# A four-branch encoder trunk in split float32: merged products reordered, down projections accumulated onto 2h in PSUM, a later first quad, and other PSUM banks

## The chip, the cores and the metric

The kernel runs on one core of a Trainium2 chip. The metric is the device time of one execution in microseconds, the median of several. A profile of one execution goes with it: for every instruction of the five engines (PE, the matrix engine, with its weight loads PEld; DVE, the vector engine; ACT, the scalar engine; POOL; SP) its start, its duration and what it waited for.

## The reference

```python
D_MODEL, SEQ, DEPTH, D_FF, CONV_DIM, N_HEADS = 1024, 512, 2, 2816, 512, 8
for i in range(DEPTH):
    h = h + 0.5 * swiglu(rmsnorm(h, ffn1_norm[i]), ffn1_w_gu[i], ffn1_w_down[i])
    u = rmsnorm(h, mix_norm[i])
    b_g, c_g, v_c, q_c, kv_c, k_r, g_conv, g_mla = split(u @ w_in[i])
    y_conv = (b_g * causal_conv3(c_g * v_c)) @ w_conv_out[i]
    y_mla = mla_branch(q_c, kv_c, k_r, ...)         # 8 heads, rotary keys, chunk mask
    h = h + (sigmoid(g_conv) * y_conv + sigmoid(g_mla) * y_mla) @ w_o[i]
    h = h + 0.5 * swiglu(rmsnorm(h, ffn2_norm[i]), ffn2_w_gu[i], ffn2_w_down[i])
    h = h + sigmoid(rmsnorm(h, ple_norm[i]) @ w_ple_gate[i]) * (p[i] @ w_ple_proj[i])
return rmsnorm(h, final_norm)
# swiglu(x): g, u = split(x @ w_gu); (silu(g) * u) @ w_down
```

All of it is float32, for 512 frames of 1024 channels.

## The kernel before

**Numbers and tiles.** `h` stands in SBUF as eight tiles of 128 channels by 512 frames. Every product is done in split precision: a value is the sum of a high and a low part (`wh`, `wl` for weights; `...h`, `...l` for activations), and `mm3` adds three matmuls, high by high (line 279), high by low (280), low by high (281), into one PSUM bank of 512 float32 columns. Weights come in blocks of 128 by 1024 (eight 128x128 tiles), by a DMA on SP's queue into one of ten buffers `st`. ACT makes the high part of a block (line 71) and DVE the low part (line 72). There are four buffers for each of the two, so a block is split at most four blocks ahead of the PE.

**Quads.** Most columns of the FFN's gate and up weights, and the mixer's gates, go through a seven-product scheme for 2x2 blocks (`Sevens`). A quad `n` makes four 128-column groups. Its seven products are named 1 to 7 and are run by `step(n, j)`. DVE forms sums of weight quarters (lines 150 to 168, tiles `st` and `s`) and of activations (`Halved.row`: for each of four `j` the sums `t` and `u` and their splits). Products 1, 2, 4, 6, and also 3 where the quad isn't "early", are merged ones, done by `joint`: for each of eight pairs of k and w, a 512-column matmul of the high weights with both parts of the activation (line 530) and then a 256-column matmul of the low weights (line 532). Products 5 and 7 (and an early 3) are done by `product` with 24 matmuls of 256 columns (line 542). ACT copies a chain's partial sum from one PSUM tile to another so that two results go on from it: `seed`, line 548. `out` and `finish` turn a result into activations.

**FFN.** `ffn(l, nm, name, first, beside, early)` is called as a0 and a1 (first FFN of layers 0 and 1) and b0, b1 (second). There are 22 column groups: in a0 four of them are done as whole products (`n_whole = 4`) and nine quads follow; in a1 it is two and ten quads; in b0 and b1 all eleven are quads, and the first two are early. `next_quad(n)` runs the rest of quad `n` among the first products of quad `n + 1`. At the places marked `None`, `fill()` puts in one down projection `down(m, f0, f0 + 4)`: twelve matmuls of 512 columns into a bank, which DVE then adds at half weight to `h[m]` (line 665). The last downs close the FFN. In a0, `beside` is `rotary`, which makes the cosine and sine tables: two DMAs on ACT's queue, 27 DVE instructions (lines 417 to 437) and two on ACT. It is called once, between the last downs.

**Mixer, per-layer embedding.** `mixer(l)` (tiles m0, m1) does the key/value and query latents (`kvp`, `qp`), the conv branch (`Cp`, `Vp`, `Bp` for k = 0 to 3), four quads of gates, then attention (`Pair`: `q_rope`, `keys_queries`, `values`; `scores`; `turn`; `mix_v`). `ple(l)` (tiles e0) does gate and projection for eight m, each pair into two banks.

**PSUM.** There are eight banks. `banks.paired()` makes three pools: `chain` (`PB`: two tiles of two banks), `seeded` (`PA`: one tile of two banks) and `single` (`PS`: two banks). `banks.eight()` makes eight single banks, for attention. A tile of a new pool waits until the old tile on its bank has been read.

**Order.** The program is traced in the order of the Python code. A planner then orders each engine's instructions at compile time, by that order as priority and by its own estimates of when data and buffers are there. On the chip each engine runs its list in order.

Of the kernel before, what the change touches and what calls it, by code (L numbers as in the profile page):

```python
# [16 lines left out]
P = 128  # L17
# [176 lines left out]
def trunk_kernel(ctx, tc, dims, x, p, positions, gains, rope_c, final_row, weights, out):  # L194
# [79 lines left out]
            nc.scalar.activation(hi, src, AF.Copy, scale=scale)  # L274
            return nc.vector.scalar_tensor_tensor(lo, src, scale, hi.bitcast(F32), ALU.mult, ALU.subtract)

    def mm3(ps, w, v, first, last):
        (wh, wl), (vh, vl) = w, v
        nc.tensor.matmul(ps, wh, vh, start=first, stop=False)  # L279
        nc.tensor.matmul(ps, wh, vl, start=False, stop=False)  # L280
        nc.tensor.matmul(ps, wl, vh, start=False, stop=last)  # L281

    def proj(tiles, vs, name, ps=None):
        ps = PS(name) if ps is None else ps
# [126 lines left out]
    def rotary():  # L411
        rc = cp.tile([P, 2], F32, tag="rc", name="rc")
        nc.scalar.dma_start(out=rc, in_=rope_c)
        pos_i = gp.tile([P, S], I32, tag="g", name="pos_i")
        nc.scalar.dma_start(out=pos_i, in_=positions.to_broadcast([P, S]))
# [5 lines left out]
        nc.vector.tensor_scalar(turns, ang, 1.0 / (2 * math.pi), None, ALU.mult)  # L421
        nc.vector.tensor_scalar(big, turns, 2.0 ** -15, magic, ALU.mult, ALU.add)
        nc.vector.tensor_scalar(big, big, magic, None, ALU.subtract)
        nc.vector.scalar_tensor_tensor(turns, big, -(2.0 ** 15), turns, ALU.mult, ALU.add)
        nc.vector.tensor_scalar(sml, turns, magic, None, ALU.add)
        nc.vector.tensor_scalar(sml, sml, magic, None, ALU.subtract)
        c2 = TWO_PI_PARTS
        for n_, c_ in ((big, c2[0] * 2 ** 15), (big, c2[1] * 2 ** 15), (sml, c2[0]), (big, c2[2] * 2 ** 15), (sml, c2[1]),
                       (big, c2[3] * 2 ** 15), (sml, c2[2]), (big, c2[4] * 2 ** 15), (sml, c2[3])):
            nc.vector.scalar_tensor_tensor(ang, n_, -c_, ang, ALU.mult, ALU.add)  # L430
        nc.vector.tensor_scalar(big, ang, 1.0 / (2 * math.pi), magic, ALU.mult, ALU.add)
        nc.vector.tensor_scalar(big, big, magic, None, ALU.subtract)
        for c_ in c2[:3]:
            nc.vector.scalar_tensor_tensor(ang, big, -c_, ang, ALU.mult, ALU.add)
        lim = 3.1415925
        nc.vector.tensor_scalar(ang, ang, lim, -lim, ALU.min, ALU.max)
        nc.vector.scalar_tensor_tensor(big, ang, -1.0, ang, ALU.mult, ALU.min)
        nc.scalar.activation(cosT, big, AF.Sin, bias=hpi)
        nc.scalar.activation(sinT, ang, AF.Sin, scale=rc[:, 1:2])

# [55 lines left out]
    class Sevens:  # L496
# [27 lines left out]
        def joint(self, ps, d, j):  # L524

            hi, lo = d.pop(("part", j), None) or d["w"].part(j)
            for k, (vh, pair) in enumerate(self.ys[j]):
                for w in range(2):
                    at = slice((2 * k + w) * P, (2 * k + w + 1) * P)
                    nc.tensor.matmul(ps[:, w, :].rearrange("p (a t) -> p a t", t=self.H), hi[:, at], pair, start=j == 1 and k == 0,  # L530
                                     stop=False, skip_group_check=True)
                    nc.tensor.matmul(ps[:, w, :self.H], lo[:, at], vh, start=False, stop=k == 3, skip_group_check=True)

        def product(self, ps, d, j, start=False):

# [68 lines left out]

    def ffn(l, nm, name, first=False, beside=None, early=2):

        H = S // 2
        nf = DFF // P
# [50 lines left out]

        def down(m, f0, f1, ps=None, last=True, first_=True):  # L660
            ps = PS(f"{name}pd{f0}_{m}") if ps is None else ps
            for f in range(f0, f1):
                mm3(ps, W.get((nm + "_w_down", l, f * P, m * P)), acts[f], first_ and f == f0, last and f == f1 - 1)
            if last:
                nc.vector.scalar_tensor_tensor(h[m], ps, 0.5, h[m], ALU.mult, ALU.add)  # L665
            return ps

        np_ = nf // 2
# [19 lines left out]
        if n_whole == 0:  # L688
            x_ins, sums = ys.other(KD // 2 - 1, xs)

            with tc.issue_after(x_ins):
                step(0, 1)
                step(0, 5)
            r = rms(acc, D, name)
            with tc.issue_after(x_ins):
                step(1, 1)
                step(1, 5)
            behind = sums
            for n, j in ((0, 2), (0, 6), (0, 3), (0, 7), (1, 2), (0, 4), (1, 6), (1, 3), (1, 7)):
                with tc.issue_after(behind):  # L700
# [3 lines left out]
        else:  # L704
# [19 lines left out]
                ys.row(j, xs)  # L724
            activate(n_whole - 2)
            f = n_whole - 1
            step(n0, 1)
            pss[f] = [proj(cs[f][0], xs, f"{name}pg{f}")]
            step(n0, 2)
            step(n0, 6)  # L730
            pss[f].append(proj(cs[f][1], xs, f"{name}pu{f}"))
            step(n0, 5)
            activate(f)
            step(n0, 7)
            step(n0, 3)
            if first:
                downs.extend((m, 0) for m in range(KD))
        for n in range(n0, np_ - 1):
            next_quad(n)

# [28 lines left out]
    def mixer(l):  # L769
# [296 lines left out]
    def ple(l):  # L1066
# [11 lines left out]
            nc.vector.tensor_tensor(h[m], h[m], g, ALU.add)  # L1078

        for m in range(KD):  # L1080
            pg, pp = halves((PA if m % 3 == 2 else PB)(f"{name}gp{m}"))
            proj(W.col("w_ple_gate", l, m * P, D), xs, None, pg)
            proj(W.col("w_ple_proj", l, m * P, PD), pt, None, pp)
            pss.append((pg, pp))
# [165 lines left out]
                store(1, 0, hg[1], nc.sync)  # L1250

    for l in range(DEPTH):
        ffn(l, "ffn1", f"a{l}", l == 0, rotary if l == 0 else None, 2 if l else 0)
        mixer(l)
        ffn(l, "ffn2", f"b{l}", early=3)
        (ple_last if l == DEPTH - 1 else ple)(l)
# [48 lines left out]
```

## Time and profile before

| | |
|---|---|
| median of 3 runs | 2321.09 us (2320.75 to 2321.31) |
| the profiled execution | 2320.87 us, of which the span from first to last instruction is 2318.8 us |
| PE busy | 2273.8 us, 98% (12272 matmuls) |
| PE weight loads | 1960.4 us, 85% |
| DVE busy | 1853.1 us, 80% |
| ACT busy | 1270.3 us, 55% |
| DMA | 223.06 MB, mean 96 GB/s |
| mean granted PE clock | 0.993 |

A matmul's row shows more than its share of the PE, since the next one starts before it ends: the times between starts tell the rate, and a stall is seen as a gap that the profile marks "idle before" with what ended it. The granted clock is 1 nearly throughout and 0.5 in short stretches.

### The profile page before, as it was taken

Reading aid. Unit: us, or ns where it says so; the run is one execution under the profiler, and the core shown is the slowest. Engines: PE = TensorE matmul, PEld = TensorE weight load, DVE = VectorE, ACT = ScalarE, POOL = GpSimd, SP = SyncE. Lnnn points to the kernel's source line nnn. Section 1 sums busy time; section 2 is a strip of 40 time slices with the busy share of each in tenths; the row PEclk is TensorE's granted clock in tenths of the full one; section 3 lists DMA queues with packets and bytes.
Section 4 is the critical chain, followed back from the end, with each engine's and each line's share of the span. In section 5 each row is a group of like instructions: output and inputs, shape, how many; then the busy total and the mean of one; then the engine's idle time right before and its main releaser. Section 6 shows DMA issues by size and latency. Waiting matters only on the chain.

```text
span 2318.8 us, 31379 instructions
## 1 busy us (share of the span) xinstructions
PE 2273.8 (98%) x12272; PEld 1960.4 (85%) x12272; DVE 1853.1 (80%) x2628; ACT 1270.3 (55%) x1922; POOL 40.4 (2%) x42
## 2 busy tenths in 40 slices
PE   8999998999999999999999999999999999999998
PEld 6888887888888788888888888888888888888887
DVE  8788877887777898887798888778888679888866
ACT  7554544466654654554665555555567465554554
POOL 0000000000110000000000000000001000000000
PEclk9999999999999999999999999999999999999999
DMA  5233342133122233334223323322221313332330
GB/s 200 91 101 100 109 132 82 64 100 100 46 84 80 73 110 100 110 100 136 82 73 109 110 100 100 127 91 83 91 83 59 106 37 118 109 102 99 107 103 37
DMA packets 63363, 223.06 MB, mean 96 GB/s; under 512 B 7280, under 2 KB 7280, under 8 KB 63216
## 3 DMA queue, kind: packets, MB, share of 16 engines
q1 hardware_dynamic: 62640, 220.28, 28.4%
q8 instruction: 96, 1.57, 0.3%
q10 hardware_dynamic: 576, 0.79, 0.1%
q14 instruction: 51, 0.42, 0.1%
HBM read 218.94 MB, written 2.10 MB: 95 GB/s over the span
## 4 chain that ended last, share of the span: by engine, by line
PE 90%; DVE 6%; ACT 2%; issue 1%; DMA 0%; SPq 0%; ACTq 0%; DVEq 0%
PE a1pd L279 2%; PE b1pd L279 2%; PE b0pd L279 2%; PE a1pd L281 2%; PE b1pd L281 2%; PE b0pd L281 2%; PE a1pd L280 2%; PE b1pd L280 2%; PE b0pd L280 2%; DVE wl L72 2%; PE a0pd L279 1%; PE a0pd L280 1%; PE a0pd L281 1%; PE e0gp L279 1%; PE e0gp L280 1%; PE e0gp L281 1%
## 5 line engine op out<-in xcount | busy, mean ns | idle before, releaser
L71 ACT CAST wh<-st 128x1024 fp32r<-128x1024 f32 (+1 forms) x503 | 524.7, 1046 | 658.6 <-PE a1pd L280 23.1
L72 DVE TENSOR_TENSOR wl<-st,wh 128x1024 fp32r<-128x1024 f32 (+1 forms) x504 | 611.2, 1214 | 253.8 <-ACT wh L71 252.9
L71 ACT CAST wh<-s 128x1024 fp32r<-128x1024 f32 x53 | 55.7, 1051 | 71.7 <-DVE s L158 4.0
L72 DVE TENSOR_TENSOR wl<-s,wh 128x1024 fp32r<-128x1024 f32 x53 | 64.7, 1221 | 11.6 <-ACT wh L71 11.4
L150 DVE TENSOR_TENSOR st<-st,s 128x1024 f32<-128x1024 f32 x49 | 59.7, 1219 | 0.0
L163 DVE TENSOR_TENSOR st<-st,st 128x1024 f32<-128x1024 f32 x45 | 55.1, 1225 | 1.3
L165 DVE TENSOR_TENSOR s<-st,st 128x1024 f32<-128x1024 f32 x45 | 54.9, 1219 | 0.1
L168 DVE TENSOR_TENSOR st<-st,st 128x1024 f32<-128x1024 f32 x45 | 54.9, 1221 | 0.0
L665 DVE SCALAR_TENSOR_TENSOR h<-a1pd,h 128x512 f32<-128x512 f32 x41 | 28.2, 689 | 6.6 <-PE a1pd L281 5.7
L665 DVE SCALAR_TENSOR_TENSOR h<-b1pd,h 128x512 f32<-128x512 f32 x41 | 28.2, 689 | 5.5 <-PE b1pd L281 4.5
L665 DVE SCALAR_TENSOR_TENSOR h<-b0pd,h 128x512 f32<-128x512 f32 x41 | 28.2, 689 | 4.5 <-PE b0pd L281 3.6
L665 DVE SCALAR_TENSOR_TENSOR h<-a0pd,h 128x512 f32<-128x512 f32 x40 | 27.6, 689 | 2.2 <-PE a0pd L281 1.3
L108 POOL MEMSET wh<- 128x256 f32 x4 | 1.1, 312 | 1214.9 <-ACT wh L71 842.5
L530 PE MATMUL a02b<-a0u,wh 128*128 128x512 f32 x16 | 8.0, 521 | 7.4 <-DVE a0u L272 7.4
L1117 PE MATMUL e1pg<-kh,e1x 128*128 128x512 f32 (+1 forms) x40 | 13.9, 349 | 0.0
L279 PE MATMUL m0Cp<-m0x,wh 128*128 128x512 f32 x32 | 12.7, 396 | 1.2 <-DVE m0qt L788 0.8
L1118 PE MATMUL e1pg<-kl,e1x 128*128 128x512 f32 (+1 forms) x40 | 13.9, 347 | 0.0
L1119 PE MATMUL e1pg<-kh,e1x 128*128 128x512 f32 (+1 forms) x40 | 13.9, 347 | 0.0
L274 ACT ACTIVATE b0x<-h,cols 128x512 fp32r<-128x512 f32 x8 | 5.8, 726 | 14.3 <-DVE h L1055 14.2
L274 ACT ACTIVATE b1x<-h,cols 128x512 fp32r<-128x512 f32 x8 | 5.8, 724 | 14.4 <-DVE h L1055 14.2
L279 PE MATMUL m1Cp<-m1x,wh 128*128 128x512 f32 x32 | 12.7, 395 | 0.7 <-DVE m1b L867 0.4
L281 PE MATMUL m0kvp<-m0x,wl 128*128 128x512 f32 x16 | 7.4, 464 | 5.9 <-DVE wl L72 5.9
(6541 smaller groups left out, 8161.5 us busy)
## 6 DMA issues: line engine op xcount, KB each, us to landing
st<-in_weights SPq DMA_DIRECT2D x406, 512.0 KB, 3.3
h<-in_x SPq DMA_DIRECT2D x8, 256.0 KB, 5.5
st<-in_weights SPq DMA_DIRECT2D x7, 256.0 KB, 5.5
out<-e1d SPq DMA_DIRECT2D x4, 256.0 KB, 2.1
out<-fh SPq DMA_DIRECT2D x3, 256.0 KB, 2.2
e0pi<-in_p SPq DMA_DIRECT2D x2, 256.0 KB, 3.6
e1pi<-in_p SPq DMA_DIRECT2D x2, 256.0 KB, 3.8
fg<-in_final_row SPq DMA_DIRECT2D x2, 256.0 KB, 4.6
```

The lines of the kernel that those rows point to most:

```text
L71: self.nc.scalar.copy(hi[:, w], src[:, w])
L72: last = self.nc.vector.tensor_tensor(lo[:, w], src[:, w], hi[:, w].bitcast(F32), ALU.subtract)
L150: tt(self.a12, self.a12, self.s, ALU.subtract)
L163: tt(self.a11, self.a11, self.a21, ALU.subtract)
L165: tt(self.s, self.a22, self.a11, ALU.subtract)
L168: tt(self.a21, self.a21, self.a22, ALU.add)
L279: nc.tensor.matmul(ps, wh, vh, start=first, stop=False)
L280: nc.tensor.matmul(ps, wh, vl, start=False, stop=False)
L281: nc.tensor.matmul(ps, wl, vh, start=False, stop=last)
L665: nc.vector.scalar_tensor_tensor(h[m], ps, 0.5, h[m], ALU.mult, ALU.add)
L1117: nc.tensor.matmul(o, vh[:, toks(t)], wh, start=first, stop=False)
L1118: nc.tensor.matmul(o, vh[:, toks(t)], wl, start=False, stop=False)
```

## The change

1. `joint` does its eight 512-column matmuls first and then its eight 256-column matmuls.
2. `down` no longer starts a sum: ACT writes `2 * h[m]` into the bank first, all matmuls add to it, and ACT writes `0.5 * bank` to `h[m]`. DVE's instruction on line 665 goes. (`mm3` gets a flag that leaves out a check of the accumulation group.)
3. In a0 the fourth whole column group is done before the first quad, into a pair of banks from `PB`, and the first four downs go among the first quad's products.
4. `rotary` becomes a generator, of which each step of `next_quad` takes one piece.
5. Early quads: the copy `seed(0, "a")` isn't made in step 1 but after the first two products of quad 1, and the norm's sum (`rms`) of b0 and b1 goes to a half of the `PA` tile in place of a `PS` bank.
6. `Cp` of k = 0 to 2 goes to a half of a `PB` tile in place of a `PS` bank.
7. `banks.eight()` comes after `pairs[0].keys_queries()`.
8. In `ple` the pairs of banks go PB, PB, PA, PS+PS, and so on, in place of PB, PB, PA.

```diff
-    def mm3(ps, w, v, first, last):
+    def mm3(ps, w, v, first, last, seeded=False):
...
     def rotary():
...
         nc.vector.tensor_copy(ang, pos_i)
+        yield
         nc.vector.tensor_scalar(ang, ang, rc[:, 0:1], None, ALU.mult)
+        yield
...
     def joint(self, ps, d, j):
-            for k, (vh, pair) in enumerate(self.ys[j]):
+            at = [slice(i * P, (i + 1) * P) for i in range(8)]
+            for k, (_, pair) in enumerate(self.ys[j]):
                 for w in range(2):
-                    at = slice((2 * k + w) * P, (2 * k + w + 1) * P)
-                    nc.tensor.matmul(ps[:, w, :].rearrange("p (a t) -> p a t", t=self.H), hi[:, at], pair, start=j == 1 and k == 0,
-                                     stop=False, skip_group_check=True)
-                    nc.tensor.matmul(ps[:, w, :self.H], lo[:, at], vh, start=False, stop=k == 3, skip_group_check=True)
+                    nc.tensor.matmul(ps[:, w, :].rearrange("p (a t) -> p a t", t=self.H), hi[:, at[2 * k + w]], pair,
+                                     start=j == 1 and k == 0, stop=False, skip_group_check=True)
+            for k, (vh, _) in enumerate(self.ys[j]):
+                for w in range(2):
+                    nc.tensor.matmul(ps[:, w, :self.H], lo[:, at[2 * k + w]], vh, start=False, stop=k == 3, skip_group_check=True)
...
     def step(self, n, j):
-                if not (early and n):
+                if not early:
                     self.seed(n, "a")
...
         def down(m, f0, f1, ps=None, last=True, first_=True):
             ps = PS(f"{name}pd{f0}_{m}") if ps is None else ps
+            if first_:
+                nc.scalar.mul(ps, h[m], 2.0)
             for f in range(f0, f1):
-                mm3(ps, W.get((nm + "_w_down", l, f * P, m * P)), acts[f], first_ and f == f0, last and f == f1 - 1)
+                mm3(ps, W.get((nm + "_w_down", l, f * P, m * P)), acts[f], False, last and f == f1 - 1, True)
             if last:
-                nc.vector.scalar_tensor_tensor(h[m], ps, 0.5, h[m], ALU.mult, ALU.add)
+                nc.scalar.mul(h[m], ps, 0.5)
...
             for i, j in enumerate((1, None, 4, 2, None, 6, None, 5, 7, 3, None)):
+                next(beside, None)
...
                 step(0, 5)
-            r = rms(acc, D, name)
+            r = rms(acc, D, name, ps=halves(PA(name + "ps"))[0])
             with tc.issue_after(x_ins):
                 step(1, 1)
                 step(1, 5)
+                sevens.seed(0, "a")
...
             if first:
+                pss[f] = whole(f)
+                projs(cs[f], xs, pss[f])
+                step(n0, 1)
+                activate(f)
                 downs.extend((m, 0) for m in range(KD))
+                for j in (2, 6, 5, 7, 3):
+                    if j in (2, 6, 5):
+                        fill()
+                    step(n0, j)
+            else:
+                step(n0, 1)
+                pss[f] = [proj(cs[f][0], xs, f"{name}pg{f}")]
+                step(n0, 2)
+                ...
+            fill()
...
-        if beside:
-            beside()
+        for _ in beside:
+            pass
...
-            ps = proj(W.col("w_in", l, o_c + k * P, D), xs, f"{name}Cp{k}")
+            pc = PS(f"{name}Cp{k}") if last else halves(PB(f"{name}Cp{k}"))[0]
+            ps = proj(W.col("w_in", l, o_c + k * P, D), xs, None, pc)
...
         step(n_last, 4)
-        banks.eight()
...
         pairs[0].keys_queries()
+        banks.eight()
         pairs[0].values()
...
-            pg, pp = halves((PA if m % 3 == 2 else PB)(f"{name}gp{m}"))
+            pg, pp = [PS(f"{name}{w}{m}") for w in ("pg", "pp")] if m % 4 == 3 else halves((PA if m % 4 == 2 else PB)(f"{name}gp{m}"))
```

More of the change, by code (lines that the diff above doesn't have):

```diff
@@ L275, in split_to @@
             return nc.vector.scalar_tensor_tensor(lo, src, scale, hi.bitcast(F32), ALU.mult, ALU.subtract)
-    def mm3(ps, w, v, first, last):
+    def mm3(ps, w, v, first, last, seeded=False):
         (wh, wl), (vh, vl) = w, v
-        nc.tensor.matmul(ps, wh, vh, start=first, stop=False)
-        nc.tensor.matmul(ps, wh, vl, start=False, stop=False)
-        nc.tensor.matmul(ps, wl, vh, start=False, stop=last)
+        nc.tensor.matmul(ps, wh, vh, start=first, stop=False, skip_group_check=seeded)
+        nc.tensor.matmul(ps, wh, vl, start=False, stop=False, skip_group_check=seeded)
+        nc.tensor.matmul(ps, wl, vh, start=False, stop=last, skip_group_check=seeded)
     def proj(tiles, vs, name, ps=None):
@@ L421, in rotary @@
         nc.vector.tensor_scalar(turns, ang, 1.0 / (2 * math.pi), None, ALU.mult)
+        yield
         nc.vector.tensor_scalar(big, turns, 2.0 ** -15, magic, ALU.mult, ALU.add)
+        yield
         nc.vector.tensor_scalar(big, big, magic, None, ALU.subtract)
+        yield
         nc.vector.scalar_tensor_tensor(turns, big, -(2.0 ** 15), turns, ALU.mult, ALU.add)
+        yield
         nc.vector.tensor_scalar(sml, turns, magic, None, ALU.add)
+        yield
         nc.vector.tensor_scalar(sml, sml, magic, None, ALU.subtract)
+        yield
         c2 = TWO_PI_PARTS
+        yield
         for n_, c_ in ((big, c2[0] * 2 ** 15), (big, c2[1] * 2 ** 15), (sml, c2[0]), (big, c2[2] * 2 ** 15), (sml, c2[1]),
@@ L430, in rotary @@
             nc.vector.scalar_tensor_tensor(ang, n_, -c_, ang, ALU.mult, ALU.add)
+            yield
         nc.vector.tensor_scalar(big, ang, 1.0 / (2 * math.pi), magic, ALU.mult, ALU.add)
+        yield
         nc.vector.tensor_scalar(big, big, magic, None, ALU.subtract)
+        yield
         for c_ in c2[:3]:
             nc.vector.scalar_tensor_tensor(ang, big, -c_, ang, ALU.mult, ALU.add)
+            yield
         lim = 3.1415925
         nc.vector.tensor_scalar(ang, ang, lim, -lim, ALU.min, ALU.max)
+        yield
         nc.vector.scalar_tensor_tensor(big, ang, -1.0, ang, ALU.mult, ALU.min)
+        yield
         nc.scalar.activation(cosT, big, AF.Sin, bias=hpi)
@@ L603, in step, with ffn @@
                 self.out(n, d.pop("b"), 1, 0)
-    def ffn(l, nm, name, first=False, beside=None, early=2):
+    def ffn(l, nm, name, first=False, beside=iter(()), early=2):
         H = S // 2
@@ L726, in ffn @@
             f = n_whole - 1
[L727 to L735, printed above, removed]
             if first:
+                pss[f] = whole(f)
+                projs(cs[f], xs, pss[f])
+                step(n0, 1)
+                activate(f)
                 downs.extend((m, 0) for m in range(KD))
+                for j in (2, 6, 5, 7, 3):
[6 more added lines that the diff above has]
+                step(n0, 2)
+                step(n0, 6)
+                pss[f].append(proj(cs[f][1], xs, f"{name}pu{f}"))
+                step(n0, 5)
+                activate(f)
+                step(n0, 7)
+                step(n0, 3)
+            fill()
         for n in range(n0, np_ - 1):
@@ L1252, in trunk_kernel @@
     for l in range(DEPTH):
-        ffn(l, "ffn1", f"a{l}", l == 0, rotary if l == 0 else None, 2 if l else 0)
+        ffn(l, "ffn1", f"a{l}", l == 0, rotary() if l == 0 else iter(()), 2 if l else 0)
         mixer(l)
```

## The prediction

> **What bounds the kernel now.** First the page: busy times, the busy tenths of the PE, and the chain that ended last.
>
> ```profile
> PE 2273.8 (98%) x12272; PEld 1960.4 (85%) x12272; DVE 1853.1 (80%) x2628; ACT 1270.3 (55%) x1922; POOL 40.4 (2%) x42
> PE   8999998999999999999999999999999999999998
> PE 90%; DVE 6%; ACT 2%; issue 1%; DMA 0%; SPq 0%; ACTq 0%; DVEq 0%
> ```
>
> The PE is the bound. An edit gains only if it shortens a train of matmuls or fills one of the 45 us (2318.8 less 2273.8) in which the PE stands. Next I list whom the PE waits for (us in total, times, longest), then cut the span into stretches around those places: width, busy time of PE, PEld, DVE, ACT and POOL, granted clock, DMA.
>
> ```profile
> PE a02b L530 <- DVE a0u L272: 7.4, 4, 2.7
> PE m0kvp L281 <- DVE wl L72: 5.9, 1, 5.9
> PE m0h0kn L279 <- DVE m0g3o L553: 3.5, 1, 3.5
> PE b11c L542 <- ACT b1ms L363: 1.8, 1, 1.8
> PE b01c L542 <- ACT b0ms L363: 1.8, 1, 1.8
> PE e0gp L279 <- DVE e0g L1077: 1.4, 1, 1.4
> PE a02a L530 <- ACT a02a L548: 1.1, 1, 1.1
> PE m0Cp L279 <- DVE m0qt L788: 0.8, 1, 0.8
> ```
>
> ```profile
> 39.00:62.00 23.00, 14.49 (x57) 10.90 (x56) 19.87 (x39) 16.63 (x28) 0.00 (x0) 0.78 0.15 47
> 362.00:379.00 17.00, 10.57 (x35) 7.87 (x34) 12.70 (x18) 5.47 (x9) 0.56 (x2) 0.80 0.36 123
> 403.00:440.00 37.00, 35.76 (x157) 28.97 (x156) 26.64 (x40) 18.45 (x27) 0.00 (x0) 1.00 0.26 86
> 571.00:582.00 11.00, 7.53 (x30) 5.85 (x29) 7.03 (x10) 7.66 (x14) 0.00 (x0) 0.84 0.41 131
> 772.00:823.00 51.00, 44.73 (x266) 38.24 (x265) 45.63 (x57) 31.66 (x44) 0.00 (x0) 0.97 0.29 93
> 1135.00:1139.00 4.00, 2.57 (x12) 1.82 (x11) 2.56 (x6) 2.43 (x3) 0.00 (x0) 1.00 0.41 131
> 1139.00:1544.00 405.00, 405.00 (x2185) 349.57 (x2184) 332.45 (x430) 221.80 (x309) 0.56 (x2) 1.00 0.30 101
> 1544.00:1581.00 37.00, 36.28 (x159) 29.39 (x158) 26.63 (x39) 18.11 (x27) 0.00 (x0) 1.00 0.26 85
> 1907.00:1959.00 52.00, 45.92 (x273) 39.32 (x272) 46.18 (x58) 32.71 (x45) 0.00 (x0) 0.97 0.29 92
> ```
>
> Width less PE busy is idle time: 8.5, 6.4, 1.2, 3.5, 6.3, 1.4, 0, 0.7 and 6.1, in all 34.1 of the 45 us. A clock under 1 is a second loss, (1 - clock) times the width: 5.1, 3.4, 1.8, 1.5 and 1.6 us, 13.4 in all, since matmuls there run at half rate. So 47.5 us hang on eight places, and the edits touch every one. The row without a loss, 1139 to 1544, holds all of a1 and the start of m1: the same FFN, with steps and downs interleaved and DVE at 82%, costs the PE nothing.
>
> **1. Merged products, 512 columns first.** Starts of matmuls tell the rate. A merged product, then a train of 512, then a train of 256, then the twelve 512s that follow a merged product:
>
> ```profile
> 302.17 0.39 PE L530 MATMUL a09b<-a0u,wh 128*128 128x512 f32 x1
> ...
> 304.98 0.40 PE L530 MATMUL a010a<-a0x,wh 128*128 128x512 f32 x1
> ```
>
> ```profile
> 326.10 0.39 PE L279 MATMUL a0pd<-a0a14h,wh 128*128 128x512 f32 x1
> ...
> 330.18 0.39 PE L530 MATMUL a010b<-a0u,wh 128*128 128x512 f32 x1
> ```
>
> ```profile
> 313.36 0.40 PE L279 MATMUL a0pd<-a0a12h,wh 128*128 128x512 f32 x1
> ...
> 316.15 0.28 PE L542 MATMUL a010d<-a0t0h,wh 128*128 128x256 f32 x1
> ...
> 319.02 0.28 PE L542 MATMUL a010b<-a0t0h,wh 128*128 128x256 f32 x1
> ```
>
> The merged product takes 2.81 us for eight pairs. A pure train of 512s goes at 4.08/18 = 0.2267 us each, a pure train of 256s at 2.87/24 = 0.1196. Eight and eight make 2.77: 0.04 less. The twelve 512s after an alternating product take 2.79 where twelve at 0.2267 take 2.72: another 0.07 that the alternation leaves behind. How much of it stays after a run of 256s no row shows: the ends are 0.04 and 0.11, and I take 0.045, near the low end, since a 256 train too runs over half of a 512's pitch. The count, and that of two other lines (stretch, width, then PE or ACT or DVE busy): lines 530, 548 and 665.
>
> ```profile
> 0.00:2318.80 2318.80, 690.70 (x1928) 363.38 (x1928) 0.99 0.29 96
> 0.00:2318.80 2318.80, 94.36 (x94) 0.99 0.29 96
> 0.00:2318.80 2318.80, 112.04 (x163) 0.99 0.29 96
> ```
>
> 1928 / 8 = 241 merged products: **-10.5 us** (ends 0 and -26). The low parts are also needed only 1.8 us later (eight times 0.2267), which helps where DVE is late; I count that under 5.
>
> [...]
>
> **2. First quad of a0 later** (39 to 62). The PE ran dry because product 6 needs four rows of activation sums, made one after another:
>
> ```profile
> 42.64 0.42 DVE L466 TENSOR_TENSOR a0t<-a0x 128x256 f32<-128x256 f32 x1
> ...
> 57.78 0.76 DVE L272 TENSOR_TENSOR a0u<-a0u,a0u 128x256 fp32r<-128x256 f32 x2
> ```
>
> The whole group couldn't fill in: its `PS` banks were held by group 2, whose reading comes after the rows. With `PB` banks its 48 matmuls (10.9 us at 0.2267) come first, from about 39.5 to 50.4; then products 1 and 2 to 56; product 6 again waits for the rows. These end at 58.5 today, and two more weight splits come before them. So 2.5 to 5 us stay, and a us or two for copies, since the first downs need `acts[3]`, behind the rows on DVE. The place costs 8.5 + 5.1 = 13.6; I take **-7.5** (ends 0 and -13.6). Its loads only change places on SP's queue, where DMA is at 0.15. The downs are moved, not added.
>
> **3. Rotary in pieces** (362 to 379). DVE before it:
>
> ```profile
> 340.00:369.00 29.00, 26.90 (x48) 1.00 0.11 38
> L430 DVE SCALAR_TENSOR_TENSOR ang<-turn_b,ang 128x512 f32<-128x512 f32 x5 | 3.4, 690 | 0.0
> L421 DVE TENSOR_SCALAR turns<-ang 128x512 f32<-128x512 f32 x1 | 0.4, 420 | 0.0
> 338.44 0.34 ACTq L415 DMA_DIRECT2D pos_i<-in_positions  x1
> ```
>
> By these, 27 pieces, 15 like L430 and 12 like L421, are about 15 us of DVE between the norm's instructions, and `kvp` waits 5.9 us for a weight split queued behind them. Layer 1's same place is in the row without a loss. The 9.8 us (6.4 + 3.4) go, bar a little: -8.5. The pieces go one per step over 2.5 quads, in which DVE has this room:
>
> ```profile
> 182.00:332.00 150.00, 150.00 (x857) 131.29 (x856) 121.01 (x149) 75.74 (x103) 0.00 (x0) 1.00 0.35 114
> 1096.00:1116.00 20.00, 20.00 (x89) 16.36 (x88) 16.52 (x24) 11.71 (x18) 0.00 (x0) 1.00 0.34 113
> ```
>
> DVE has 29 us free in 150, or 15 in the 77 us of 2.5 quads, and the downs' leaving gives back ten times 0.69. It is tight: +1 (ends 0 and +6). The two DMAs take ACT's queue 0.34 us each, behind nothing urgent. Net **-7.5** (ends 0 and -9.8).
>
> **4. `Cp` banks**: 1.2 + 0.7 idle at 403 to 440 and 1544 to 1581, all waits for DVE to read a bank. `Cp` now uses `PB` tiles read long before, `Vp` and `Bp` have the two `PS` banks for themselves: **-2** (ends 0, -2).
>
> **5. Early quads** (772 to 823, 1907 to 1959). The 1.8 us wait was quad 1's `c` for the bank that the norm's sum held until ACT read it; now it has its own. The clock loss of 1.5 behind it goes too. Afterwards DVE is the limit (45.6 of 51 us busy); it will start earlier by what the PE gains, since it waited for weights there too. The moved seed needs the `PA` tile free and 1 us of ACT (94.36/94) within the 5.7 us of products 1 and 5. I take 3.0 of 3.3 for each layer: **-6** (ends 0 and -15.4, all idle and clock).
>
> **6. Eight banks later**: the 3.5 us wait for the last gate's bank goes, with 1.8 of clock. Price: four products on two `PS` banks, so the second key and query each wait for a split of the first (0.62 on ACT, 0.69 on DVE). Layer 1, without a stall today, can only lose. 5.3 - 1.8: **-3.5** (ends +1 and -5.3).
>
> **7. `ple`**: no pair of banks comes back within three groups: **-1.4** (ends 0, -1.4).
>
> **8. Downs onto 2h.** 163 DVE instructions (112 us) leave; ACT gets 326. Nearest row:
>
> ```profile
> L271 ACT CAST m0qn<-m0qt 128x512 fp32r<-128x512 f32 x3 | 1.8, 616 | 1.5 <-PE m0g3b L532 1.4
> L665 DVE SCALAR_TENSOR_TENSOR h<-a0pd,h 128x512 f32<-128x512 f32 x8 | 5.5, 690 | 0.0
> ```
>
> 326 x 0.62 = 202 us: ACT goes from 55% to 63%, and DVE from 80% to 75%. DVE's 112 us buy nothing where the PE has no wait. New is the wait: a down can't start before its seed, the seed not before ACT has emptied that bank, and that not before the down two earlier ended. Behind it on ACT stand weight casts, of which four are done ahead, 32 tiles x 3 x 0.2267 = 22 us of downs. In the closing downs two short ones (1.4 us) must hide an emptying and a seed (1.24). The FFN's end loads ACT most: 11.7 of 20 us busy at 1096 to 1116, plus about ten of these. The 94 copies on line 548, each 1 us and each needed by the PE, cost one visible wait, 1.1 us. So **+1.5** (ends -3, if DVE's relief helps at the starts, and +10).
>
> The Trainium skill, "ScalarE: Activation LUTs", section "What ACT_TABLE_LOAD costs", gives 186 ns + 0.833 per column with immediate scale, 612 ns, the same sum; a remark there, that ACT is faster into PSUM than into SBUF, no row here shows for this form.
>
> **Sum**: -10.5 - 7.5 - 7.5 - 2 - 6 - 3.5 - 1.4 + 1.5 = -36.9. The profiled execution took 2320.87 us, 0.2 below the median 2321.09: 2284.
>
> **Rivals.** (a) *Seeds in the PE's way*, the slower side: ACT's list puts a seed behind a weight cast that itself waits for the PE. Exposed in full, 163 x 0.62 = 101 us, less 38.4: 2384. It decides from 38.4 / 163 = 0.24 us per down. Against it stand the 94 copies; for it, two banks only. (b) *DVE takes back the starts*: parts 2 and 5 give nothing and the rotary pieces cost 5 in the quads, since DVE is at 86% in 39 to 62 and 89% in 772 to 823: -10.5 - 3.5 - 2 - 3.5 - 1.4 + 1.5 = -19.4, 2301. (c) *The order in a merged product is indifferent*: without part 1 -26.4, 2294; against it the 0.04 between rows. (d) *Every stall goes*: -10.5 - 47.5, 2263; against it ACT's load and the rows of product 6.
>
> **Chances.** Forecast 0.60, with 2273 to 2296 as its own range; (a) 0.08, of which 0.05 is slower, 0.02 no change and 0.01 faster, as its size is anything from 0; (b) 0.17; (c) 0.10; (d) 0.05. Under 0.2%, 4.6 us, counts as no change, about what a measurement of this kernel can tell. Faster 0.93, same 0.02, slower 0.05. The range 2266 to 2304 leaves out (a), the upper part of (b) and most of (d), some 0.17.
>
> **What would show it.** Part 1: merged products of 2.77 us between starts, and 2.72 to 2.76 for the twelve 512s behind. Parts 2 to 7: no PE wait over 1 us on `m0kvp`, `m0h0kn`, `b01c`, `b11c`, `e0gp`, `Cp`; clock at 1 there; 2.5 to 6 us of waits left at a0's first product 6. Part 8: few PE waits on the 2h seeds, none on the closing downs over 0.5 us. Wrong if many downs wait for ACT, if DVE fills up in a0's quads 2 to 4 and the PE waits for `wl` there, or if `m1h0` shows new waits of over 1 us.

## The result, and the profile after

The changed kernel takes 2285.69 us (median of 4 runs, 2284.97 to 2286.7) against 2320.92 for the kernel before beside it: a ratio of 0.9849, interval 0.9832 to 0.9866, or 35.2 us less. The profiled execution's span fell from 2318.8 to 2284.9 us, by 33.9. Parts are numbered below as in the prediction (its parts 2 and 3 are items 3 and 4 in the list of the change, its part 8 is item 2). First, lines of the page of the changed kernel: span, busy times, the chain that ended last, and the two instructions of a down projection on ACT.

```profile
span 2284.9 us, 31443 instructions
...
PE 2254.5 (99%) x12272; PEld 1959.8 (86%) x12272; DVE 1746.8 (76%) x2465; ACT 1447.3 (63%) x2250; POOL 40.4 (2%) x42
...
PE 93%; DVE 4%; ACT 2%; issue 0%; DMA 0%; SPq 0%; ACTq 0%; DVEq 0%
...
L684 ACT ACTIVATE h<-a0pd 128x512 f32<-128x512 f32 x41 | 24.3, 597 | 23.1 <-PE a0pd L281 23.0
L680 ACT ACTIVATE a0pd<-h 128x512 f32<-128x512 f32 x41 | 24.5, 601 | 2.5 <-DVE a010o L570 1.7
```

The PE does the same 12272 matmuls. It is idle for 30.4 us instead of 45 and busy for 19.3 us less, since its matmuls stand closer and fewer of them run at half clock (mean granted clock 0.996, before 0.993). DVE lost the 163 additions. ACT took on 328 instructions, at 597 and 601 ns: there are 164 downs now, since a0 has 41 where it had 40. Next, the list of whom the PE waits for in the changed kernel (us in total, times, longest):

```profile
PE a02a L545 <- ACT a02a L565: 2.4, 1, 2.4
PE a02b L545 <- DVE a0u L272: 2.2, 1, 2.2
PE a02d L559 <- ACT a02d L565: 2.0, 1, 2.0
PE a0pd L279 <- ACT a0pd L680: 1.3, 1, 1.3
PE m0h0kn L279 <- DVE m0h0kn0l L272: 1.2, 1, 1.2
PE m1h0kn L279 <- DVE m1h0kn0l L272: 1.2, 1, 1.2
PE m1h0v L946 <- DVE m1h0qn1l L272: 1.1, 1, 1.1
...
PE b01b L545 <- ACT wh L71: 1.0, 1, 1.0
```

`m0kvp`, `b01c` and `b11c` on the norm, `e0gp` and `Cp` are gone. a0's start is still there, with other names, and attention's start in layer 1 has two waits that it didn't have. The stretches of the changed kernel that answer to those of before (width, then busy time of PE, PEld, DVE, ACT and POOL, granted clock, DMA):

```profile
39.00:66.00 27.00, 21.66 (x98) 17.64 (x96) 24.46 (x42) 18.45 (x31) 0.00 (x0) 0.94 0.18 59
66.00:82.00 16.00, 13.07 (x56) 10.07 (x57) 7.49 (x11) 8.80 (x15) 0.00 (x0) 0.89 0.19 66
340.00:369.00 29.00, 29.00 (x128) 23.61 (x127) 17.60 (x22) 22.06 (x37) 0.56 (x2) 1.00 0.27 91
395.00:432.00 37.00, 37.00 (x165) 30.61 (x164) 28.17 (x44) 19.05 (x28) 0.00 (x0) 1.00 0.25 86
555.00:573.00 18.00, 16.79 (x91) 14.10 (x91) 12.66 (x19) 12.29 (x21) 0.00 (x0) 1.00 0.33 114
757.00:808.00 51.00, 47.20 (x284) 41.93 (x284) 48.96 (x62) 34.15 (x48) 0.00 (x0) 0.97 0.35 114
1680.00:1696.00 16.00, 13.71 (x74) 11.33 (x73) 11.11 (x16) 11.96 (x21) 0.00 (x0) 1.00 0.33 116
1884.00:1935.00 51.00, 47.23 (x287) 42.19 (x286) 48.89 (x62) 33.04 (x48) 0.00 (x0) 0.97 0.37 120
```

Rows three and four are now full: the rotary stall and the `Cp` stalls. The first two lose 8.3 us of PE time and 3.4 of clock, where one stretch lost 8.5 and 5.1 before.

To add up such losses without counting one twice, I take all starts of matmuls and sum what lies between two of them beyond 226.7 ns per 512 columns: gaps over 30 ns as stalls (half clock included), the smaller ones as pitch. By this the 33.9 us are 22.9 of stalls (73.9 to 51.0) and 11.0 of pitch (50.7 to 39.7):

| part | forecast | in the trace, by starts | on the chip |
|---|---|---|---|
| 1 joints | -10.5 | pitch -11.0 | 13.2 when undone, 13.1 alone |
| 2 a0's first quad | -7.5 | 13.1 to 13.1 | 1.1 when undone (span 0.1) |
| 3 rotary pieces | -7.5 | 9.5 to 0.3 | 2.0 when undone (span 0.3), 10.3 where 8 is undone too |
| 4 `Cp` banks | -2 | 3.0 to 0 | not run alone |
| 5 early quads | -6 | 22.4 to 14.3 | 5.2 when undone (span 4.6) |
| 6 eight banks | -3.5 | m0 5.4 to 1.6, m1 0 to 2.9 | not undone in full |
| 7 `ple` | -1.4 | 1.7 to 0 | not run alone |
| 8 downs onto 2h | +1.5 | e1's `pp` 0.4 to 1.0 | 2.7 faster when undone (span 4.6) |

The middle column adds to -33.3. The profiled execution is the slowest of the four for the changed kernel and the fastest of the four with part 8 undone, so spans and medians can differ by some 2 us. The ratios below have intervals of about 0.0015 on either side, 3.5 us, so differences of 1 to 3 us rest on the traces of the places and on ranges that don't touch, not on the ratios alone.

### The profile page after: what moved, and what is told of

It is laid out like the page before. It is cut to its first block, busy times and chain, and to the rows that moved or that the text cites. A ratio compares the mean times of both kernels' runs of the same rounds, so it can differ in the third digit from the quotient of the medians.

```text
span 2284.9 us, 31443 instructions
## 1 busy us (share of the span) xinstructions
PE 2254.5 (99%) x12272; PEld 1959.8 (86%) x12272; DVE 1746.8 (76%) x2465; ACT 1447.3 (63%) x2250; POOL 40.4 (2%) x42
## 4 chain that ended last, share of the span: by engine, by line
PE 93%; DVE 4%; ACT 2%; issue 0%; DMA 0%; SPq 0%; ACTq 0%; DVEq 0%
PE a1pd L279 2%; PE b1pd L279 2%; PE b0pd L279 2%; PE b1pd L280 2%; PE a1pd L280 2%; PE b0pd L280 2%; PE a0pd L279 2%; PE b0pd L281 2%; PE a1pd L281 2%; PE b1pd L281 2%; PE a0pd L280 2%; PE a0pd L281 2%; DVE wl L72 1%; ACT wh L71 1%; PE m0mop L279 1%; PE m1mop L279 1%
## 5 line engine op out<-in xcount | busy, mean ns | idle before, releaser
L684 ACT ACTIVATE h<-a0pd 128x512 f32<-128x512 f32 x41 | 24.3, 597 | 23.1 <-PE a0pd L281 23.0
L684 ACT ACTIVATE h<-b1pd 128x512 f32<-128x512 f32 x41 | 24.4, 597 | 21.6 <-PE b1pd L281 21.6
L684 ACT ACTIVATE h<-b0pd 128x512 f32<-128x512 f32 x41 | 24.4, 597 | 21.1 <-PE b0pd L281 21.0
L684 ACT ACTIVATE h<-a1pd 128x512 f32<-128x512 f32 x41 | 24.2, 597 | 19.0 <-PE a1pd L281 18.7
L680 ACT ACTIVATE b1pd<-h 128x512 f32<-128x512 f32 x41 | 24.6, 602 | 3.5 <-DVE b110o L570 1.4
L680 ACT ACTIVATE b0pd<-h 128x512 f32<-128x512 f32 x41 | 24.6, 602 | 3.5 <-DVE b010o L570 1.4
L680 ACT ACTIVATE a0pd<-h 128x512 f32<-128x512 f32 x41 | 24.5, 601 | 2.5 <-DVE a010o L570 1.7
L680 ACT ACTIVATE a1pd<-h 128x512 f32<-128x512 f32 x41 | 24.5, 601 | 2.2 <-DVE a110o L570 1.4
L280 PE MATMUL a0p<-a0x,wh 128*128 128x512 f32 x44 | 17.2, 392 | 0.0
L281 PE MATMUL a0p<-a0x,wl 128*128 128x512 f32 x44 | 17.1, 389 | 0.0
L279 PE MATMUL a0p<-a0x,wh 128*128 128x512 f32 x44 | 17.1, 389 | 0.0
L274 ACT ACTIVATE b0x<-h,cols 128x512 fp32r<-128x512 f32 x8 | 5.8, 726 | 14.3 <-DVE h L1087 14.2
L274 ACT ACTIVATE b1x<-h,cols 128x512 fp32r<-128x512 f32 x8 | 5.8, 724 | 14.3 <-DVE h L1087 14.2
```

The costliest lines, as they stand in the source:

```text
L279: nc.tensor.matmul(ps, wh, vh, start=first, stop=False, skip_group_check=seeded)
L280: nc.tensor.matmul(ps, wh, vl, start=False, stop=False, skip_group_check=seeded)
L281: nc.tensor.matmul(ps, wl, vh, start=False, stop=last, skip_group_check=seeded)
L680: nc.scalar.mul(ps, h[m], 2.0)
L684: nc.scalar.mul(h[m], ps, 0.5)
```

## The experiments

Each diff is against the changed kernel, but for the second. The time of the changed kernel is 2285.69.

**The order of a merged product.** The old order in the changed kernel:

```diff
             for k, (vh, pair) in enumerate(self.ys[j]):
                 for w in range(2):
                     nc.tensor.matmul(ps[:, w, :]..., hi[:, at], pair, ...)
+                    nc.tensor.matmul(ps[:, w, :self.H], lo[:, at], vh, ...)
-            for k, (vh, _) in enumerate(self.ys[j]):
-                for w in range(2):
-                    nc.tensor.matmul(ps[:, w, :self.H], lo[:, at[2 * k + w]], vh, ...)
```

> The changed kernel with part 1 alone undone: 512 and 256 columns alternate again in all 241 merged products. Theory (the order is a price of its own): between starts the changed kernel has 2.77 us for a merged product and about 0.03 of slow 512s behind it, the old one 2.82 and 0.04 to 0.06; 241 times 0.045 to 0.05 is 11 us, so 2296 to 2298 us, and no new wait of over 1 us. Rival (order indifferent, the gain came from the low weight parts being needed later): about 2286, or some us more with new waits for wl in the trace. Second rival (the whole tail of 0.07 had gone too): 241 x 0.11 = 26 us, 2312.

2298.94 us, 0.9906 [0.9889, 0.9923], 0.9 above the theory's range. The span is 12.0 longer: 11.0 of pitch and 1.1 of stalls. Then the other way, the kernel before with the new order and nothing else (the same lines, reversed):

> The kernel before with part 1 alone: the eight 512-column matmuls of each merged product stand before its eight 256-column ones. Nothing else is changed. Theory: the order of widths by itself is worth 11 us over 241 products wherever the PE is not waiting: 2320.7 - 11 = 2310, range 2308 to 2312; the waits of before on m0kvp, m0h0kn, b01c, b11c and e0gp stay as they are. Rival: part of the 13.2 us that undoing it in the changed kernel cost comes from the later need of the low parts, 1.8 us later per product, which takes 1 to 2 us out of the starts of b0 and b1 besides: then 2307 to 2308 and shorter waits of the PE on DVE there. Second rival: order indifferent in this surrounding: 2320.

2307.34 us, 0.9941 [0.9927, 0.9955], 13.1 under the kernel before. The span falls by 12.3: 11.2 of pitch and 1.0 of stalls (the starts of b0 and b1 are 2.9 us shorter, others a little longer). The time lies in the first rival's range: the theory's 11 of pitch, and 1 to 2 us besides. The other waits of before are still in its list:

```profile
PE m0kvp L281 <- DVE wl L72: 5.9, 1, 5.9
...
PE b01c L544 <- ACT b0ms L363: 1.9, 1, 1.9
```

And half of the way: four of 512, four of 256, and again.

```diff
-            for k, (_, pair) in enumerate(self.ys[j]):
...
+            for g in range(2):
+                for k in (2 * g, 2 * g + 1):   # 512 columns, both w
...
+                for k in (2 * g, 2 * g + 1):   # 256 columns, both w
```

> The changed kernel with merged products in groups of four: 4x512, 4x256, 4x512, 4x256. Theory A (each 256-column matmul behind another costs 6.7 ns over half a 512's pitch, and each train of 256s leaves 27 ns of slow 512s behind it, whatever its length): two trains of four cost 2 x (20 + 27) = 94 ns a product in place of 46 + 27 = 73; 241 x 0.021 = +5 us, 2291. Theory B (a fixed price for each change from 256 back to 512: alternation has 8 changes and costs 11 us more than 1 change): +1.6 us, 2287. Theory C (any grouping does): 2285.7.

2294.18 us, 0.9885 [0.987, 0.99]: 5.6 of the span's 7.0 are pitch, the rest stalls. The pitch fits theory A, which expected 5 (the time is 3 us above its 2291), and not the 1.6 and the 0 of the others. The timeline of this kernel, one merged product (x4 stands for four matmuls in a row):

```profile
296.31 1.09 PE L546 MATMUL a09d<-a0x,wh 128*128 128x512 f32 x4
297.24 0.63 PE L550 MATMUL a09d<-a0x,wl 128*128 128x256 f32 x4
297.71 1.09 PE L546 MATMUL a09d<-a0x,wh 128*128 128x512 f32 x4
298.64 0.64 PE L550 MATMUL a09d<-a0x,wl 128*128 128x256 f32 x4
299.12 0.40 PE L279 MATMUL a0pd<-a0a12h,wh 128*128 128x512 f32 x1
```

2.81 us between starts. The first four 512s stand behind a train of 256s and take 0.93 us, where four at 0.2267 take 0.91, and the second four do so again. The changed kernel, a merged product and the twelve 512s behind it:

```profile
90.98 1.98 PE L545 MATMUL a03b<-a0x,wh 128*128 128x512 f32 x8
92.80 1.11 PE L549 MATMUL a03b<-a0x,wl 128*128 128x256 f32 x8
93.75 0.40 PE L279 MATMUL a0pd<-a0a0h,wh 128*128 128x512 f32 x1
...
96.50 1.98 PE L545 MATMUL a02b<-a0u,wh 128*128 128x512 f32 x8
```

2.77 and 2.75 us. Here the 256s go at 0.95/8 = 0.119 us, as in trains of one kind, and the first 512s behind them lose 0.027 us in all. So a run of 256s costs a little at its own pitch and a little behind it, and of the three orders the one with the fewest runs is the fastest. The new order also changes how often high and low weights take turns, but that is not the cost: the plain trains of 512s and of 256s take two matmuls with high weights and one with low in turn throughout, and they run at the 0.2267 and 0.1196 us that all this is measured against. What in the PE makes mixed widths slower no run shows.

**The order at a0's start** (part 2 undone, which the expectation calls part 3 by the list of the change: the old branch, product 1 first, the whole group's two halves between products 1, 2, 6 and 5, no downs there).

```diff
-            if first:
-                pss[f] = whole(f)
-                projs(cs[f], xs, pss[f])
-                step(n0, 1)
-                activate(f)
...
+            step(n0, 1)
+            pss[f] = [proj(cs[f][0], xs, f"{name}pg{f}")]
+            step(n0, 2)
+            step(n0, 6)
...
```

> The changed kernel with part 3 of the change alone undone: a0's fourth group again after product 1 of the first quad, on PS banks. Theory (from the trace after: the later quad gained nothing, since its stalls, 13.1 us by starts, are as large as before's): 2284 to 2287. Rival (the forecast's 7.5 us are in it, and something else at the start ate them): 2291 to 2294.

2286.76 us, 0.9855 [0.984, 0.9869], and a span within 0.1: part 2 gives nothing. The list of waits shows the two places of before (the stalls are 14.0 us by starts):

```profile
PE a02b L545 <- DVE a0u L272: 7.9, 3, 3.8
PE a02a L545 <- ACT a02a L565: 1.8, 1, 1.8
```

Why the new order gives nothing can be read in the timeline of the changed kernel. DVE (first and last row of activation sums, and a weight sum between), then ACT, then the PE:

```profile
43.46 0.42 DVE L481 TENSOR_TENSOR a0t<-a0x 128x256 f32<-128x256 f32 x1
43.79 1.22 DVE L168 TENSOR_TENSOR st<-st,st 128x1024 f32<-128x1024 f32 x1
...
63.07 0.75 DVE L272 TENSOR_TENSOR a0u<-a0u,a0u 128x256 fp32r<-128x256 f32 x2
...
53.65 0.72 ACT L480 ACTIVATE a0x<-h,cols 128x512 f32<-128x512 f32 x1
54.28 1.00 ACT L565 COPY a02a<-a02b 128x1024 f32<-128x1024 f32 x1
...
55.33 2.93 PE L545 MATMUL a02a<-a0x,wh 128*128 128x512 f32 x7 [2.37 <-ACT a02a L565]
```

The rows end at 63.8 us, where they ended at 58.5 before: the planner put six weight sums and splits, 1.22 us each, between the rows' instructions, where two splits stood before. And the PE, through with product 1 at 52.9, waits for the copy to `a02a`, which stands on ACT behind casts and the rows' own ACT instructions.

**Activations ahead of the rows.** If so, the downs' material should come first, and the rows should stand in a run:

```diff
-            for j in range(early, KD // 2):
-                ys.row(j, xs)
-            activate(n_whole - 2)
             f = n_whole - 1
             if first:
                 pss[f] = whole(f)
+                activate(n_whole - 2)
                 projs(cs[f], xs, pss[f])
-                step(n0, 1)
                 activate(f)
+                for j in range(early, KD // 2):
+                    ys.row(j, xs)
                 downs.extend((m, 0) for m in range(KD))
+                step(n0, 1)
```

> The changed kernel with another order at a0's start: groups 2 and 3 are activated ahead of the four activation rows, and the first downs stand among the first quad's products as before. Theory (the rows alone, at the head of DVE's and ACT's lists, hold back everything: the activations of groups 2 and 3, so the first downs, and the seeds on ACT; with acts first the downs fill the time of the rows): the 13.1 us of stalls by starts between 50 and 80 fall to 2 to 6, 2276 to 2281. Rival (the start is bound by DVE's sum of work, whatever the order): product 6 waits longer by what the downs wait less, 2284 to 2288.

2281.37 us, 0.9834 [0.982, 0.9849], 4.3 less than the changed kernel and the fastest of all kernels here. The theory holds in the main: the time is 0.4 above its range, and more of the stalls stay than the 2 to 6 us expected. The same two stretches in this kernel, and what still waits:

```profile
39.00:66.00 27.00, 27.00 (x126) 22.15 (x125) 24.38 (x36) 19.27 (x32) 0.00 (x0) 1.00 0.22 71
66.00:82.00 16.00, 11.48 (x60) 9.70 (x60) 13.00 (x21) 10.72 (x19) 0.00 (x0) 0.79 0.14 46
```

```profile
PE a02b L545 <- DVE a0u L272: 4.5, 2, 3.8
```

13.1 us of stalls became 7.4. The PE is full to 66 us and then waits for the rows' end on DVE, which drops the clock.

**Downs back on DVE** (part 8 undone).

```diff
-            if first_:
-                nc.scalar.mul(ps, h[m], 2.0)
...
-                nc.scalar.mul(h[m], ps, 0.5)
+                nc.vector.scalar_tensor_tensor(h[m], ps, 0.5, h[m], ALU.mult, ALU.add)
```

> The changed kernel with part 8 alone undone: downs start their own sums and DVE adds them to h. Theory of the forecast (the seeds cost 1.5 us, DVE's relief gives nothing): 2284, with the PE wait of 1.3 us on the first seed in a0 gone. Rival (DVE's 112 us of relief made part of the gain, in the DVE-filled starts of b0 and b1, in a0 and beside the rotary pieces): 2288 to 2292, with more PE waits for wl at those places and DVE back at about 80%.

2282.96 us (2282.12 to 2283.95), 0.9838 [0.9824, 0.9853]: faster than with the downs onto 2h, and the rotary stall doesn't come back. a0's start has 10.0 us of stalls instead of 13.1, `e1pp` 0.4 instead of 1.0. The starts of b0 and b1 are as they were, so DVE's relief buys nothing there. The rival falls.

**Rotary at one place again** (part 3 undone):

```diff
             for i, j in enumerate((1, None, 4, 2, None, 6, None, 5, 7, 3, None)):
-                next(beside, None)
```

> The changed kernel with the rotary tables again all at one place, between a0's last downs. Theory: the stall at m0's start comes back with its clock loss, 9.5 us by starts before, perhaps less as the downs no longer stand on DVE there (8 x 0.6 = 5 us less in front of the norm): 2290 to 2295. The pieces in the quads cost nothing in the trace after, so nothing is gained there. Rival (with the downs off DVE the tables fit between the last downs): 2285 to 2287.

2287.73 us, 0.9861 [0.9846, 0.9876]; the span is 0.3 longer and `m0kvp` doesn't wait. The rival holds (the time is 0.7 above its range). Since neither part was needed by itself, both were undone together:

> Parts 3 and 8 are both undone: the rotary tables go back to one place between a0's last downs, and the downs go back to DVE's addition behind them. All other parts stay. Known beside it: with part 3 alone undone the kernel took 2287.73 us and showed no wait on m0kvp; with part 8 alone undone it took 2282.96. Theory: either of the two keeps the stall away, because 15 us of rotary work and 69 additions of 0.69 us in one FFN are too much for DVE only together. Then the m0kvp stall of before (6.9 us at 362 to 379, and 2.6 us of half clock) comes back, and the time is 2283 + 6 to 11, 2289 to 2294 us. Rival: the stall left for another reason, such as the later low parts of the merged products, which leave DVE more time. Then no wait over 1 us on m0kvp, and 2282 to 2285 us.

2293.23 us, 0.9884 [0.9868, 0.9899], 10.3 above the kernel with part 8 alone undone. The stall is back, as the theory says. Stretch of the kernel with the late rotary and the downs on ACT, then the one with both undone, and the latter's longest wait:

```profile
335.00:365.00 30.00, 29.94 (x132) 24.34 (x131) 26.74 (x44) 23.36 (x38) 0.00 (x0) 1.00 0.18 60
```

```profile
335.00:365.00 30.00, 24.97 (x108) 19.73 (x106) 28.13 (x49) 16.07 (x25) 0.00 (x0) 0.99 0.09 32
```

```profile
PE m0kvp L281 <- DVE wl L72: 6.4, 1, 6.4
```

With the downs on ACT the whole of the rotary work fits into DVE's time and the PE stays full; with the downs on DVE it doesn't. Parts 3 and 8 are two cures for one stall.

**Early quads** (part 5 undone: the norm's sum in a `PS` bank, the copy `seed(0, "a")` in step 1).

```diff
-                if not early:
+                if not (early and n):
...
-            r = rms(acc, D, name, ps=halves(PA(name + "ps"))[0])
+            r = rms(acc, D, name)
...
-                sevens.seed(0, "a")
```

> The changed kernel with part 5 alone undone: the norm's sum of b0 and b1 on a single bank, seed(0, a) in step 1. Theory (the whole gain at b0 and b1, 8.1 us by starts, is the freed bank with the clock loss behind it, and DVE's list moves up with the PE): 2293 to 2295, the wait of 1.8 us on b01c for the norm's last reading back in both layers. Rival (half of the 8.1 us came from low parts being needed later, part 1): 2289 to 2291.

2290.89 us, 0.9874 [0.9858, 0.9891]: 5.2 more, with both waits back:

```profile
PE b01c L559 <- ACT b0ms L363: 1.9, 1, 1.9
PE b11c L559 <- ACT b1ms L363: 1.9, 1, 1.9
```

The rival that gave part 5 only a part of the 8.1 us holds; in the kernel with the new order of merged products alone the two starts are 1.4 and 1.5 us shorter too.

**Attention's first keys on other banks**: the second key and query of the first pair on the two halves of the `PA` tile.

```diff
-                ps = proj(W.col("w_ukv", ...), kvc, f"{self.n}kn{t}")
+                ps = proj(W.col("w_ukv", ...), kvc, None, self.bank(t, 0, "kn"))   # PA half for t = 1
```

> The changed kernel with the second key and query of the first pair of heads on the two halves of the free PA tile, in place of the two single banks. Theory (the PE waits there for the split of the first key, 1.2 us in either layer, and in m1 1.1 us for that of the second query): the waits on m0h0kn and m1h0kn go, and that on m1h0v with them; 2.9 + 1.6 us by starts less a rest of up to 1: 2281 to 2283. Rival (DVE is late there whatever the bank, since the rotary of the query and the last gate stand before): the wait moves to qn or v, 2285 to 2287.

2285.47 us, 0.9853 [0.9838, 0.9867]: nothing gained. The waits moved to the next use of a split of the same keys, so it is DVE that is late there, not the bank:

```profile
PE m1h0kq L279 <- DVE m1h0kn1l L272: 1.6, 1, 1.6
PE m0h0kq L279 <- DVE m0h0kn1l L272: 1.6, 1, 1.6
```

**Two combinations**: activations first, three downs instead of one ahead of product 6, and layer 1's eight banks at the old place.

```diff
-                    if j in (2, 6, 5):
+                    for _ in range({2: 1, 6: 3, 5: 1}.get(j, 0)):
                         fill()
...
+        if l:
+            banks.eight()
...
-        banks.eight()
+        if l == 0:
+            banks.eight()
```

(The weights that the expectation asks for early are those of the three `fill()`s.)

> The changed kernel, downs onto 2h kept, with three edits: in a0 the activations of groups 2 and 3 stand before the rows of weight sums; three weight copies and splits instead of one are asked for before product 6 of the first quad; and layer 1 takes the eight banks where the kernel before did, layer 0 where the changed one does. Theory: the first edit is worth the 4.3 us that it showed alone, the second takes 2 to 4 of the 4.5 us of a02b's wait on DVE and of the half clock behind it, the third the 2.9 us of waits of m1h0kn and m1h0v: 2285.7 - 4.3 - 3 - 2.9 = 2275.5, range 2274 to 2278. Rival: the three weights asked for early delay the rows on DVE and so product 6 itself; then 2279 to 2281.

2284.82 us, 0.9848 [0.9834, 0.9862]: 9 above the forecast of 2275.5, outside the rival's 2279 to 2281 too, and above the kernel with the activations first alone. This kernel's longest waits, the stretch around the first of them, and DVE and ACT at 105 us:

```profile
PE m1h0kn L279 <- DVE m1g3o L570: 4.1, 1, 4.1
PE a03d L559 <- ACT a03d L565: 1.9, 1, 1.9
```

```profile
1676.00:1692.00 16.00, 11.88 (x53) 9.74 (x52) 9.55 (x14) 11.02 (x19) 0.00 (x0) 0.89 0.31 103
```

```profile
105.76 1.22 DVE L163 TENSOR_TENSOR st<-st,st 128x1024 f32<-128x1024 f32 x1
106.90 0.68 DVE L570 TENSOR_TENSOR a03o<-a03a,a03o 128x512 f32<-128x512 f32 x1
...
107.61 1.00 ACT L565 COPY a03d<-a03b 128x1024 f32<-128x1024 f32 x1 [0.71 <-DVE a03o L570]
```

Both added edits missed. The old place of the eight banks costs 6.0 us in layer 1 (4.1 of wait, the rest half clock) where the new one costs 2.9. And more downs ahead of product 6 did take the wait for the rows away, but the same DVE is late one quad further on, at 103 to 113 us: 8.1 us of stalls to 134 us, where the activations alone leave 7.7. Then the same with the downs on DVE (part 8's diff as above):

> The kernel of the run beside it with part 8 undone: the downs are added by DVE again, so ScalarE writes no 2h. Theory: the seeds cost something only where ACT is late, at a0's start and at e1pp. With the activations first and more weights ahead, a0's start no longer depends on the seeds, and of the 2.7 to 4.6 us that undoing part 8 alone gave, 0.6 to 1.5 stay: 2274 to 2275.5 if the run beside it gives 2275.5. Rival: the seeds cost in every FFN, and the full 2.7 to 4.6 us come off: 2271 to 2273. Second rival: without ACT's help DVE fills up at a0's start; then slower than the run beside it.

2284.42 us, 0.9847 [0.9833, 0.9861]. The two differ by 0.4 us, in their spans by 1.7, of which `e1pp` has 0.6. The rival with the full 2.7 to 4.6 falls. The theory that the seeds cost only where ACT is late fits the 0.6, but 0.4 us between medians can't be told from nothing, and both kernels lie 9 to 10 us above the numbers given.

## Why the prediction was right or wrong

The time, 2284 against 2285.69, came out so close partly by luck. By the trace's column above, parts 2 and 6 gave 10.1 us less than the sum has for them, and the other six 6.5 us more; the misses offset each other. By steps:

- **Part 1 (-10.5)**: right in mechanism and size: 11.0 of pitch, 0.046 us for each of 241 products where I took 0.045 (241 times 0.045 is 10.8, not the 10.5 in the sum). What stays behind a run of 256s, which no row of before showed, is 0.027 us. 1 to 2 us came on top from the low parts' later need, which I had counted under 5. Rival (c), order indifferent, falls: sixteen matmuls take 2.77 us in one order and 2.81 in the other, and alone the order moves 13.1 us. The Trainium skill, "TensorE: Matmul & The Clock Gate", section "Back-to-back issue gap", gives the gap of an isolated warm matmul as its columns over 2.4 plus 2.5 ns; an estimate by it would be 2.60 us in either order, below both.
- **Part 2 (-7.5)**: wrong, 0. The step that failed is "these end at 58.5 today, and two more weight splits come before them", with 2.5 to 5 us left. I let the rows keep their place on DVE; the planner put weight sums and splits among them and they ended 5.3 us later. And I counted "a us or two for copies": four waits on ACT and DVE, 7.9 us and with the half clock behind them the place's 13.1. Rival (b)'s mechanism, DVE taking back the starts, was right here and only here. Part 8 has a share in it: with the downs on DVE the place has 10.0 us of stalls. Parts 2 and 8 were not undone together, so how much part 2 gives without the 2h seeds stays open.
- **Part 3 (-7.5)**: the stall went with all its 9.2 us, and the +1 for the quads didn't show, since undoing the pieces gains nothing there. But the reason that I gave, the pieces' place, is one of two; DVE's relief by part 8 does it as well.
- **Part 8 (+1.5)**: right that the seeds don't stand in the PE's way: rival (a) needed 0.24 us per down, and the whole list of waits has 1.3 us on a seed. Its price is at a0's start, where ACT also has the rows and copies: 3.1 us, and 0.6 at `e1pp`: 3.7 by the trace where I had 1.5. "DVE's 112 us buy nothing" missed that without part 3 they would buy 5.5 us (2293.23 to 2287.73).
- **Part 5 (-6)**: 5.2 by undoing it, 8.1 in the trace together with part 1. The waits on the norm went, but "clock at 1 there" failed: both stretches still have 0.97 over 51 us.
- **Part 6 (-3.5)**: -0.9 in the trace. Layer 0 came as forecast (-3.8 where I had -5.3 plus 1.8 for the new waits), but the sum has no term of its own for layer 1. There the forecast's sign of being wrong, new waits of over 1 us at `m1h0`, came up (1.2 and 1.1 us): "can only lose" came true against the kernel before, by 2.9, but not against its alternative: with the old place and the other parts in, it loses 6.0. In the kernel before, this key started at 1714.0 us without a wait, though the same reader of a gate's bank came at 1716.9; with `Cp` gone from the `PS` pool the key seems to get that reader's bank. That was read, not tried.
- **Parts 4 and 7** gave 3.0 and 1.7 by the trace, where I had 2 and 1.4. Neither was undone alone, so that the banks did it is read from the waits that went.

Rival (d), every stall gone, fell at a0, b0 and b1, where 27 us remain.

## What to carry to other kernels

In this kernel runs of matmuls of one width were cheaper than alternating widths, also behind the run; where the PE is the bound, such a reordering is worth trying. When a new order puts work in front of a chain on a busy engine, ask where the planner will put that engine's other work: here the chain itself was unchanged, and its end moved by 5 us. Two edits against one stall should be undone singly and together, since singly each looks worthless.

## What the runs showed of the hardware

The cost of mixing widths doesn't go by the number of changes: 14 changes of width more in each of the 241 merged products than the changed kernel's one cost 11.0 us of pitch, and two more already cost 5.6. And not every stall slows the clock: the 1.2 us wait at `m0h0kn` leaves it at 1.00 (555 to 573 us), while two of a0's waits (2.4 and 2.0 us), and the 4.1 us one above, are each followed by some 3.4 us at half rate (0.89 over 16 us is 3.5 us at half). That is the length of the window, 3413 ns, that the Trainium skill gives, "TensorE: Matmul & The Clock Gate", section "What's actually happening"; the trace agrees. ACT's instruction took 601 ns from SBUF into PSUM and 597 from PSUM into SBUF, so no faster way shows.
